# First column pair of the output projection as eight plain block products, and two norms turned with diagonal matrices

## The chip, the cores and the metric

The kernel runs on one core of one Trainium2 chip. The metric is the device time of one launch in microseconds; the median of three runs before the change is 2388.78 us (2388.70 to 2394.04).

The core's engines run their own queues in order and meet at semaphores: TensorE (PE, matrix products into PSUM), VectorE (DVE), ScalarE (ACT), GpSimd (POOL) and SyncE (SP, here only a queue of loads).

## The reference

One layer over 512 latent tokens of width 2048, with 256 context tokens that only feed the initial states of the scans. All arithmetic is float32.

```
mods      = silu(c) @ w_mod + b_mod                  # shift, scale, gate, twice
hx        = rmsnorm(x) * norm1_g * (1 + sc1) + sh1
q,k,v,g,… = hx @ w_in                                # heads of linear attention, and a short convolution
o         = bidirectional gated scan of q,k,v        # 4 heads, key 128, value 256, chunks of 64
mix[0:8]  = rmsnorm(o) * gla_norm_g * silu(g)        # norm over the 256 values of a head
mix[8:16] = B * conv3(C * x_in)
x1        = x + gt1 * (mix @ w_out)                  # the output projection, 2048 x 2048
h2        = rmsnorm(x1) * norm2_g * (1 + sc2) + sh2
out       = rmsnorm(x1 + gt2 * ((silu(h2 @ w_gate) * (h2 @ w_up)) @ w_down)) * final_g
```

## The kernel before

**Split products.** Every large float32 product is three products of two parts: `hi` is the value rounded to PE's faster float format (L102, a cast on ACT), `lo` is the rest (L103, a subtraction on DVE), and `mm3` adds lo·hi, hi·lo and hi·hi in PSUM. So each weight tile of 128 x 1024 (512 KB) costs one cast and one subtraction before PE may use it. The parts have three buffers each (`whi`, `wlo`); raw weights have four (`raw`, `load_raw`).

**First half: projections and scans.** `hx` is kept as 16 column tiles with their parts; the odd ones lie in the eight buffers tagged `ch`, the even ones in the 32 tagged `h`. `proj_units` multiplies one weight tile with eight of these, 24 matmuls, and yields. `do_q`, `do_g` and `do_conv` are built of such units. `do_gla(h)` is the scan of a head, cut by yields into steps. `weave` runs one step of the scan and one projection unit in turn until the scan is done, and then the rest of the units, so that PE always has a unit between two steps. After each unit `mod_some(MOD_STEP, 64)` adds 0.95 of a modulation row: a row is two loads of 512 KB through the `raw` buffers and two multiply-and-sum instructions on DVE (L373). The units of all `weave` calls are 74 steps. `mod_some(64, 64)` does what is left at the end, and `mod_finish` makes `modv`, from which the gates of the projections come (`cols_to_row`, two small turns on PE at L841).

At the end of a scan the norm of a head (L629 to L634) squares each 128 x 256 part of the output on ACT with a sum per row, makes the reciprocal root (`rsqrt_of_sum`, seven small instructions on DVE and ACT), and scales the parts with it on ACT. One yield later PE turns them in blocks of 128 x 128 (L639), tokens along the free axis, and DVE multiplies with `silu(g)` into `mix` (L641).

**Second half: products in seven.** The output projection and both FFN products multiply blocks by the Strassen-Winograd form: the left matrix is cut in four (`A11`, `A12`, `A21`, `A22`: token half and half of the inner dimension), the right one too, and seven products with sums of blocks take the place of eight. The left operands are `A11`, `A12`, `A22` and the sums `S1 = A21 + A22`, `S2 = S1 - A11`, `S3 = A11 - A21`, `S4 = A12 - S2`. `prep_a` makes and splits them, group after group. `seven` runs the products in steps named by block ("1", "5", "63", "7", "24"); `before` holds functions that are called ahead of a step. For each of four units of a product there are 12 matmuls of 128 x 512. `after` takes the finished sums. For the output projection `w_out` is two column pairs, `p = 0` and `p = 1`, and `prep_a` is called once, ahead of both; `take` multiplies by the gate row, adds `x`, squares for the second norm, and stores the sum to DRAM on POOL's queue. `load_x` loads the gate rows and `x` ahead of step "63".

The first half of the tokens is normalised before step "7" of the second pair (`half_a`), the second half after it: `norm2_scale` makes the root and scales eight tiles on ACT (L878), `norm2_back` turns them (L888, 32 turns of 128 x 128) and applies scale and shift on ACT (L893). The left operands of the FFN for the second half are made ahead of step "5" of the FFN's first block column, `j = 0` (`half_b`).

**Order and buffers.** The order on PE, DVE, ACT and POOL is set by a planner that takes instructions in the order of the text when its own costs say that their operands are ready; from the output projection on, SP's loads keep the order of the text. Tiles share buffers by tag: `t` (24 in `xpool`, where the 16 `mix` tiles lie too), `h` (32), `e` (17), `ch` (8); a tile waits for the last use of the one whose buffer it takes.

Of the kernel before, what the change touches and what calls it, by code (L numbers as in the profile page):

```python
# [7 lines left out]
F32 = mybir.dt.float32  # L8
# [5 lines left out]
P = 128  # L14
# [8 lines left out]
DV = 256  # L23
# [30 lines left out]
def tile_hybrid_block(  # L54
# [76 lines left out]
    def tok(t, tt):  # L131
        return t[:, tt * P : tt * P + P]
# [18 lines left out]
    def row_bcast(ps, pool, r):  # L151

        for tt in range(r.shape[-1]):
            dg = pool.tile([P, P], F32, tag="rb_d", name="rb_d", bufs=2)
            nc.vector.tensor_scalar(dg, ident, r[:, tt : tt + 1], None, op0=ALU.mult)
            mm(tok(ps, tt), ones, dg, tt == 0, True)


# [219 lines left out]

    MOD_STEP = 0.95

# [174 lines left out]
    def do_gla(h):  # L555
# [8 lines left out]
        for d in range(2):  # L564
# [64 lines left out]
        for tt in range(NX):  # L629
            nc.scalar.activation(on[:, tt, :], opart(tt), AF.Square, accum_out=ss[:, tt : tt + 1])  # L630
        r = rsqrt_of_sum(gp, ss, 1.0 / DV, NX)
        for tt in range(NX):
            nc.scalar.activation(on[:, tt, :], opart(tt), AF.Copy, scale=r[:, tt : tt + 1])
        yield  # L634

        for vh in range(2):
            pt = bank("pt")
            for tt in range(NX):
                nc.tensor.transpose(tok(pt, tt), on[:, tt, vh * P : vh * P + P], ident)  # L639
            m = mix[2 * h + vh]  # L640
            nc.vector.scalar_tensor_tensor(m, pt, col(C_GLA + vh), m, op0=ALU.mult, op1=ALU.mult)  # L641
# [48 lines left out]
    ctx.enter_context(tc.manual_schedule(engines={mybir.EngineType.SP}))  # L690
    A11, S1, S2, S4, S3, A12, A22 = range(7)

# [6 lines left out]
    def new_a(nk):  # L699

        return [[None] * (nk // 2) for _ in range(7)]

    def a_unit(A, i, u, spill=()):
        if A[i][u] is None:
            A[i][u] = tuple(fpool.tile([P, 2, HALF], F32R, tag="e", name=f"a{i}{p}", bufs=17) if (i, u) in spill else
                            xpool.tile([P, 2, HALF], F32R, tag="h" if i < 4 else "t", name=f"a{i}{p}",
                                       bufs=32 if i < 4 else 24) for p in "hl")
        return A[i][u]

    def prep_a(A, pieces, order, spill=()):  # L710


        tmp = {}
        tt = nc.vector.tensor_tensor

        def put(u, sel, i, src):
            hi, lo = a_unit(A, i, u, spill)
            split(hi[:, sel, :], lo[:, sel, :], src)

        def one(i, u, sel, a11, a12, a21, a22):  # L720
            if i == S1:
                if u not in tmp:
                    tmp[u] = row2k("s").rearrange("p (k t) -> p k t", k=2)
                tt(tmp[u][:, sel, :], a21(), a22(), op=ALU.add)
            elif i == S2:
                tt(tmp[u][:, sel, :], tmp[u][:, sel, :], a11(), op=ALU.subtract)
            elif i == S4:
                tt(tmp[u][:, sel, :], a12(), tmp[u][:, sel, :], op=ALU.subtract)
            if i == S3:
                t = row2k("s3").rearrange("p (k t) -> p k t", k=2)[:, sel, :]  # L730
                tt(t, a11(), a21(), op=ALU.subtract)
                put(u, sel, i, t)
            elif i in (S1, S2, S4):
                put(u, sel, i, tmp[u][:, sel, :])
            else:
                put(u, sel, i, {A11: a11, A12: a12, A22: a22}[i]())

        for group in order:
            for piece in pieces:
                for i in group if type(group) is tuple else (group,):  # L740
                    one(i, *piece)
            yield

    ALL_STEPS = ("1", "5", "63", "7", "24")

    def seven(A, wsrc, nk, after, steps=ALL_STEPS, before={}):
# [23 lines left out]
        for step in steps:  # L770
            if step in before:
                before[step]()
            for u in range(nu):
                end = u == nu - 1
                if step == "1":
# [36 lines left out]
    def sums(take, roomy=False):  # L812
# [18 lines left out]
        def direct(acc):  # L831
            for t in range(2):
# [23 lines left out]
    mx = lambda i, hf: (lambda: mix[i][:, hf * HALF : hf * HALF + HALF])  # L856
    for _ in prep_a(A, [(n // 2, n % 2, mx(k, 0), mx(l, 0), mx(k, 1), mx(l, 1)) for n, (k, l) in enumerate(zip(MIX1, MIX2))],
                    (A11, S1, S2, S4, S3, (A12, A22)), spill=((A22, 2), (A22, 3))):
        pass
    xn = [[None] * NBD for _ in range(NX)]  # L860
# [9 lines left out]

    raws, xs = {}, {}

    def norm2_scale(hf):
        r = row_scale(ssq, 2 * hf, 2)
        for d in range(NBD):
            for t in range(2):
                xs[2 * hf + t, d] = big() if hf else hbig()
                nc.scalar.activation(xs[2 * hf + t, d], xn[2 * hf + t][d], AF.Copy, scale=r[:, t : t + 1])  # L878
# [19 lines left out]
    rw = lambda hf, u: (lambda: raws[hf, u])  # L898
    gen = prep_a(A2, [(u, ALL, rw(0, u), rw(0, 4 + u), rw(1, u), rw(1, 4 + u)) for u in range(4)],
                 (A11, A12, S1, S2, S3, S4, A22))  # L900

    def half_a():
        norm2_scale(0)
        norm2_back(0)
        next(gen)
        next(gen)

    for p in range(NBD // 2):
# [19 lines left out]

        before = {"63": load_x}
        if p:  # L930
            before["7"] = half_a
        seven(A, lambda b, u: wo[p, b, u], 8, sums(take, True), ("1", "5", "63", "2", "7", "4") if p else ALL_STEPS, before)

# [5 lines left out]
    acts = {}  # L939

    def half_b():
        norm2_back(1)
        for _ in gen:
            pass

# [45 lines left out]
    for j in range(NPU):  # L991
# [15 lines left out]
        if j == 0:  # L1007
            steps, before = ("1", "2", "5", "63", "7", "4"), {"5": half_b}
        else:
# [199 lines left out]
```

## Time and profile before

| | |
|---|---|
| median of three runs | 2388.78 us (2388.70 to 2394.04) |
| profiled execution | 2393.07 us, its span 2391.3 us |
| mean granted clock of PE | 0.973 |
| busy in the span | PE 2252.2 us, DVE 1704.9, ACT 1030.8, POOL 136.3 |
| loads and stores | 431.42 MB, 180 GB/s on average |
| scans begin (first head's turn of k, L559) | 419.90 us |
| first matmul of the output projection | 849.45 us |
| first matmul of its second pair | 955.87 us |
| first matmul of the FFN, and of its second block column | 1053.46 and 1155.46 us |

Times within the profile count from the start of the span. A line of the waits says which engine's instruction stood idle for which, with the total, the number of times and the longest. A line of groups has the busy time, the mean length of one in ns, and the idle time in front. A line of the timeline has start and length; `x8` are eight instructions in a row, and brackets hold the idle time in front and what ended it. PE's rows overlap their neighbours, so the work of one is read from start to start. A product of two plain float32 operands leaves two rows.

### The profile page before, as it was taken

The numbers are of one execution on the slowest core, as the hardware profiler recorded it, in microseconds if no ns is written. First come the engines' busy times: TensorE is split into PE (matmuls) and PEld (weight loads), VectorE is DVE, ScalarE is ACT, GpSimd is POOL, SyncE is SP. The second block draws the span as 40 slices with busy tenths as digits, with TensorE's granted clock in tenths as the row PEclk, the third lists the DMA queues.
The fourth block names the chain that finished last, engine by engine and source line by source line (L and its number), as shares of the span: only waits on it lengthen the run. The fifth ranks groups of instructions, "written<-read, shape, count | busy, mean of one in ns | idle before, by whom it ended". The sixth has DMA issues, their size and how long they took to land.

```text
span 2391.3 us, 27558 instructions
## 1 busy us (share of the span) xinstructions
PE 2252.2 (94%) x10184; PEld 1793.0 (75%) x10184; DVE 1704.9 (71%) x2088; ACT 1030.8 (43%) x1391; POOL 136.3 (6%) x186
## 2 busy tenths in 40 slices
PE   8999999888979969987999999999999999999996
PEld 4765666777868747765888888888888878888875
DVE  3555165665665577768887888788877867787798
ACT  3422055322232344475445554555454544443343
POOL 2422000000000000000000000000000000000001
PEclk9999999999989989998999999999999999999998
DMA  9773466665766244541446434544354494855734
GB/s 326 229 253 111 150 228 194 199 213 187 231 192 217 90 150 128 178 157 52 145 150 203 143 128 145 193 150 142 139 176 159 165 362 151 289 185 178 255 130 141
DMA packets 161619, 431.42 MB, mean 180 GB/s; under 512 B 17867, under 2 KB 38635, under 8 KB 161356
## 3 DMA queue, kind: packets, MB, share of 16 engines
q1 hardware_dynamic: 141612, 380.87, 48.1%
q0 software_dynamic: 8720, 28.58, 3.2%
q10 hardware_dynamic: 11152, 20.21, 2.3%
q8 instruction: 80, 1.31, 0.2%
q14 instruction: 55, 0.45, 0.1%
HBM read 380.82 MB, written 48.78 MB: 180 GB/s over the span
## 4 chain that ended last, share of the span: by engine, by line
issue 57%; POOL 2%; PE 2%; DVE 0%; POOLq 0%; ACT 0%
PE acc L90 2%; POOL opd L971 2%; POOL out L1088 0%; POOL xnd L927 0%; ACT whi L102 0%; DVE xn L925 0%; POOLq L971 0%; DVE wlo L103 0%; DVE u L924 0%; DVE g L922 0%; DVE u L827 0%; POOLq L1205 0%; POOLq L1088 0%; POOLq L927 0%
## 5 line engine op out<-in xcount | busy, mean ns | idle before, releaser
L102 ACT CAST whi<-ch 128x1024 fp32r<-128x1024 f32 x370 | 390.2, 1056 | 461.5 <-PE acc L90 380.4
L103 DVE TENSOR_TENSOR wlo<-ch,whi 128x1024 fp32r<-128x1024 f32 x370 | 450.5, 1224 | 153.8 <-ACT whi L102 153.0
L102 ACT CAST whi<-raw 128x1024 fp32r<-128x1024 f32 x244 | 256.4, 1053 | 405.7 <-PE acc L90 284.9
L103 DVE TENSOR_TENSOR wlo<-raw,whi 128x1024 fp32r<-128x1024 f32 x244 | 302.5, 1240 | 158.8 <-ACT whi L102 158.1
L373 DVE CUSTOM_DVE_ANT_0 raw<-raw,cbc 128x1024 f32<-128x1024 f32 x128 | 156.3, 1224 | 159.6 <-DMA raw<-wm 157.2
L90 PE MATMUL acc<-hhl,whi 128*128 128x512 f32 x640 | 200.0, 393 | 0.0
L90 PE MATMUL acc<-hhi,wlo 128*128 128x512 f32 x320 | 133.4, 418 | 9.1 <-DVE wlo L103 8.3
L90 PEld LDWEIGHTS acc<-hhl,whi 128*128 128x128 f32 x640 | 121.1, 190 | 27.3 <-issue 2.5
L90 PE MATMUL acc<-wlo,a0h 128*128 128x512 f32 x296 | 117.5, 397 | 25.1 <-DVE wlo L103 25.1
L90 PE MATMUL acc<-hhl,wlo 128*128 128x512 f32 x320 | 127.5, 398 | 0.0
L90 PE MATMUL acc<-hlo,whi 128*128 128x512 f32 x320 | 127.2, 397 | 0.2 <-DVE hlo L108 0.2
L90 PE MATMUL acc<-hhi,whi 128*128 128x512 f32 x320 | 126.8, 396 | 0.0
L90 PE MATMUL acc<-whi,a1l 128*128 128x512 f32 x296 | 117.3, 398 | 9.6 <-DVE a1l L103 8.0
L90 PE MATMUL acc<-wlo,a1h 128*128 128x512 f32 x296 | 117.2, 396 | 9.5 <-DVE wlo L103 9.5
L90 PE MATMUL acc<-whi,a6l 128*128 128x512 f32 x296 | 116.4, 395 | 8.8 <-ACT whi L102 7.5
L90 PE MATMUL acc<-whi,a2l 128*128 128x512 f32 x296 | 116.1, 395 | 6.4 <-ACT whi L102 6.4
L90 PE MATMUL acc<-wlo,a2h 128*128 128x512 f32 x296 | 118.0, 399 | 0.9 <-DVE wlo L103 0.9
L90 PE MATMUL acc<-whi,a2h 128*128 128x512 f32 x296 | 117.8, 398 | 0.0
L90 PE MATMUL acc<-wlo,a6h 128*128 128x512 f32 x296 | 116.6, 394 | 0.9 <-DVE wlo L103 0.9
L90 PE MATMUL acc<-whi,a1h 128*128 128x512 f32 x296 | 116.9, 395 | 0.0
L90 PE MATMUL acc<-wlo,a3h 128*128 128x512 f32 x296 | 115.6, 391 | 1.1 <-DVE wlo L103 1.1
L90 PE MATMUL acc<-wlo,a4h 128*128 128x512 f32 x296 | 115.4, 390 | 1.2 <-DVE wlo L103 1.2
(310 smaller groups left out, 4802.8 us busy)
## 6 DMA issues: line engine op xcount, KB each, us to landing
raw<-wm SPq DMA_DIRECT2D x128, 512.0 KB, 4.7
raw<-wu SPq DMA_DIRECT2D x92, 512.0 KB, 4.5
ch<-wu SPq DMA_DIRECT2D x88, 512.0 KB, 3.8
raw<-wc SPq DMA_DIRECT2D x48, 512.0 KB, 3.7
raw<-wd SPq DMA_DIRECT2D x47, 512.0 KB, 6.4
ch<-wd SPq DMA_DIRECT2D x44, 512.0 KB, 6.0
opd<-oh ACTq DMA_DIRECT2D x77, 256.0 KB, 3.1
opd<-ol POOLq DMA_DIRECT2D x77, 256.0 KB, 3.3
```

Of the source, the lines that this page charges most:

```text
L90: nc.tensor.matmul(o, l, r, start=start, stop=stop, skip_group_check=True)
L102: nc.scalar.copy(hi, src)
L103: (eng or nc.vector).tensor_tensor(lo, src, hi, op=ALU.subtract)
L373: nc.vector.tensor_tensor_reduce(out=w, in0=w, in1=cbc[:, hf * 1024 : hf * 1024 + 1024], scale=1.0, scalar=0.0, op0=ALU.mult, op1=ALU.add, ...
L971: nc.gpsimd.dma_start(opd[j][i, 1].rearrange("p k t -> p (k t)"), lo.bitcast(F32))
```

## The change

- **Output projection, first pair.** `seven` with `p = 0` becomes `eight`: for each of the two columns, both halves of the inner dimension and four units, 24 matmuls into four banks. Its weights go through `raw`, where `seven` held the first two blocks in `ch`. The left blocks are made unit by unit (`hooks`): `A11` and `A21` ahead of the first half, `A12` and `A22` ahead of the second, and the sums for the second pair in the second column. `A21` and the raw sums lie in `ch`, `A12`, `A22` and `S2` in `h`, `S3`, `S4` and half of `S1` in `t`, the rest of `S1` in `e`.
- **Norm of a head.** The parts are copied to SBUF as they are and squared in place in PSUM. After a yield the root is made, and from it four diagonal matrices on DVE (`diagonals`); after two more yields PE multiplies the parts with them, which scales and turns at once.
- **Second norm.** The eight scaled copies of `norm2_scale` go; two diagonal matrices of a half take their place, and the turns of `norm2_back` become products with them. The second half's turns stand ahead of step "2" of `j = 0`, and its left operands are made unit by unit.
- `do_gla` yields once more before the scores (`psc`), and `MOD_STEP` is 0.85.

```diff
+    def diagonals(pool, r, bufs=4):
+        dgs = []
+        for tt in range(r.shape[-1]):
+            dg = pool.tile([P, P], F32, tag="dg", name="dg", bufs=bufs)
+            nc.vector.tensor_scalar(dg, ident, r[:, tt : tt + 1], None, op0=ALU.mult)
+            dgs.append(dg)
+        return dgs
...
-    MOD_STEP = 0.95
+    MOD_STEP = 0.85
...
             kes.append(ke)
             yield
+        yield
         for d in range(2):
             psc = bank("psc")
...
         for tt in range(NX):
-            nc.scalar.activation(on[:, tt, :], opart(tt), AF.Square, accum_out=ss[:, tt : tt + 1])
-        r = rsqrt_of_sum(gp, ss, 1.0 / DV, NX)
-        for tt in range(NX):
-            nc.scalar.activation(on[:, tt, :], opart(tt), AF.Copy, scale=r[:, tt : tt + 1])
+            nc.scalar.copy(on[:, tt, :], opart(tt))
+            nc.scalar.activation(opart(tt), opart(tt), AF.Square, accum_out=ss[:, tt : tt + 1])
+        yield
+        dgs = diagonals(gp, rsqrt_of_sum(gp, ss, 1.0 / DV, NX))
+        yield
         yield
...
-                nc.tensor.transpose(tok(pt, tt), on[:, tt, vh * P : vh * P + P], ident)
+                mm(tok(pt, tt), on[:, tt, vh * P : vh * P + P], dgs[tt], tt == 0, True)
...
+    def eight(A, wsrc, nk, take, before={}):
+        nu = nk // 2
+        for c in range(2):
+            acc = [[bank8("acc"), bank8("acc")] for _ in range(2)]
+            for kh in range(2):
+                for u in range(nu):
+                    if (c, kh, u) in before:
+                        before[c, kh, u]()
+                    hi = wpool.tile([P, 1024], F32R, tag="whi", name="whi", bufs=3)
+                    lo = wpool.tile([P, 1024], F32R, tag="wlo", name="wlo", bufs=3)
+                    split(hi, lo, load_raw(wsrc(2 * kh + c, u)))
+                    for hf in range(2):
+                        for t in range(2):
+                            for k in range(2):
+                                mm3(acc[hf][t], sl(A[((A11, A12), (A21, A22))[hf][kh]][u], ALL, k, slice(t * P, t * P + P)),
+                                    (hi[:, k * NB : k * NB + NB], lo[:, k * NB : k * NB + NB]),
+                                    kh == 0 and u == 0 and k == 0, kh == 1 and u == nu - 1 and k == 1)
+            for tt in range(NX):
+                take(tt, c, None, acc[tt // 2][tt % 2])
...
-    for _ in prep_a(A, [...], (A11, S1, S2, S4, S3, (A12, A22)), spill=((A22, 2), (A22, 3))):
-        pass
+    prep = preparer(A, pieces, lambda: wpool.tile([P, 2 * NB], F32, tag="ch", name="s", bufs=8)[:, :NB],
+                    lambda i, u: {A21: "ch", S1: "e" if u < 2 else "t", S3: "t", S4: "t"}.get(i, "h"))
...
     def norm2_scale(hf):
-        r = row_scale(ssq, 2 * hf, 2)
-        for d in range(NBD):
-            for t in range(2):
-                xs[2 * hf + t, d] = big() if hf else hbig()
-                nc.scalar.activation(xs[2 * hf + t, d], xn[2 * hf + t][d], AF.Copy, scale=r[:, t : t + 1])
+        dgs2[hf] = diagonals(fpool, row_scale(ssq, 2 * hf, 2), 3)
...
-            dst = row2k("h2") if hf else hbig()
+            dst = row2k("h2") if hf else big()
...
-                    nc.tensor.transpose(pt[:, (2 * kk + t) * P : (2 * kk + t) * P + P],
-                                        xs[2 * hf + t, k // 4][:, k % 4 * P : k % 4 * P + P], ident)
+                    mm(pt[:, (2 * kk + t) * P : (2 * kk + t) * P + P],
+                       xn[2 * hf + t][k // 4][:, k % 4 * P : k % 4 * P + P], dgs2[hf][t], kk == 0 and t == 0, True)
...
+        if p == 0:
+            before = hooks(prep, ((0, 0), (A11, A21)), ((0, 1), (A12, A22)), ((1, 0), (S1, S3)), ((1, 1), (S2, S4)))
+            first = before[0, 1, 0]
+            before[0, 1, 0] = lambda: (first(), load_x())
+            eight(A, w, 8, take, before)
+        else:
+            seven(A, w, 8, sums(take, True), ("1", "5", "63", "2", "7", "4"), {"63": load_x, "7": half_a})
...
         if j == 0:
-            steps, before = ("1", "2", "5", "63", "7", "4"), {"5": half_b}
+            steps = ("1", "2", "5", "63", "7", "4")
+            before = hooks(prep2, (("5",), (S1,)), (("63",), (S2, S4)), (("7",), (S3,)), (("4",), (A22,)))
+            before["2"] = lambda: norm2_back(1)
```

More of the change, by code (lines that the diff above doesn't have):

```diff
@@ L690, in tile_hybrid_block @@
     ctx.enter_context(tc.manual_schedule(engines={mybir.EngineType.SP}))
-    A11, S1, S2, S4, S3, A12, A22 = range(7)
+    A11, S1, S2, S4, S3, A12, A22, A21 = range(8)
     def bank8(name="bank8"):
@@ L699, in new_a, with a_unit @@
     def new_a(nk):
-        return [[None] * (nk // 2) for _ in range(7)]
-    def a_unit(A, i, u, spill=()):
+        return [[None] * (nk // 2) for _ in range(8)]
+    def a_unit(A, i, u, home=None):
         if A[i][u] is None:
-            A[i][u] = tuple(fpool.tile([P, 2, HALF], F32R, tag="e", name=f"a{i}{p}", bufs=17) if (i, u) in spill else
-                            xpool.tile([P, 2, HALF], F32R, tag="h" if i < 4 else "t", name=f"a{i}{p}",
-                                       bufs=32 if i < 4 else 24) for p in "hl")
+            home = home(i, u) if home else "h" if i < 4 else "t"
+            if home == "ch":
+                both = wpool.tile([P, 2, 2, HALF], F32R, tag="ch", name=f"a{i}", bufs=8)
+                A[i][u] = (both[:, 0], both[:, 1])
+            else:
+                pool, bufs = {"h": (xpool, 32), "t": (xpool, 24), "e": (fpool, 17)}[home]
+                A[i][u] = tuple(pool.tile([P, 2, HALF], F32R, tag=home, name=f"a{i}{p}", bufs=bufs) for p in "hl")
@@ L708, in a_unit, with preparer @@
         return A[i][u]
-    def prep_a(A, pieces, order, spill=()):
+    def preparer(A, pieces, sum_tile, home=None):
         tmp = {}
         tt = nc.vector.tensor_tensor
[L716 to L742, printed above, removed]
@@ new lines, in do @@
+        def do(u, *ops):
+            for i in ops:
+                hi, lo = a_unit(A, i, u, home)
+                if i == S1:
+                    tmp[u] = sum_tile().rearrange("p (k t) -> p k t", k=2)
+                t = row2k("s3").rearrange("p (k t) -> p k t", k=2) if i == S3 else tmp.get(u)
+                for sel, a11, a12, a21, a22 in pieces[u]:
+                    if i == S1:
+                        tt(t[:, sel, :], a21(), a22(), op=ALU.add)
+                    elif i == S2:
+                        tt(t[:, sel, :], t[:, sel, :], a11(), op=ALU.subtract)
+                    elif i == S4:
+                        tt(t[:, sel, :], a12(), t[:, sel, :], op=ALU.subtract)
+                    elif i == S3:
+                        tt(t[:, sel, :], a11(), a21(), op=ALU.subtract)
+                    else:
+                        split(hi[:, sel, :], lo[:, sel, :], {A11: a11, A12: a12, A21: a21, A22: a22}[i]())
+                if i in (S1, S2, S3, S4):
+                    split(hi, lo, t)
@@ L744, in tile_hybrid_block @@
+        return do
     ALL_STEPS = ("1", "5", "63", "7", "24")
@@ L773, in seven @@
             for u in range(nu):
+                if (step, u) in before:
+                    before[step, u]()
                 end = u == nu - 1
@@ L856, in tile_hybrid_block @@
     mx = lambda i, hf: (lambda: mix[i][:, hf * HALF : hf * HALF + HALF])
-    for _ in prep_a(A, [(n // 2, n % 2, mx(k, 0), mx(l, 0), mx(k, 1), mx(l, 1)) for n, (k, l) in enumerate(zip(MIX1, MIX2))],
-                    (A11, S1, S2, S4, S3, (A12, A22)), spill=((A22, 2), (A22, 3))):
-        pass
+    pieces = [[(n % 2, mx(MIX1[n], 0), mx(MIX2[n], 0), mx(MIX1[n], 1), mx(MIX2[n], 1)) for n in (2 * u, 2 * u + 1)]
+              for u in range(4)]
+    prep = preparer(A, pieces, lambda: wpool.tile([P, 2 * NB], F32, tag="ch", name="s", bufs=8)[:, :NB],
+                    lambda i, u: {A21: "ch", S1: "e" if u < 2 else "t", S3: "t", S4: "t"}.get(i, "h"))
     xn = [[None] * NBD for _ in range(NX)]
@@ L869, in row_scale @@
         return rsqrt_of_sum(fpool, s, 1.0 / D, n)
-    raws, xs = {}, {}
+    raws, dgs2 = {}, {}
     def norm2_scale(hf):
-        r = row_scale(ssq, 2 * hf, 2)
-        for d in range(NBD):
-            for t in range(2):
-                xs[2 * hf + t, d] = big() if hf else hbig()
-                nc.scalar.activation(xs[2 * hf + t, d], xn[2 * hf + t][d], AF.Copy, scale=r[:, t : t + 1])
+        dgs2[hf] = diagonals(fpool, row_scale(ssq, 2 * hf, 2), 3)
     def norm2_back(hf):
@@ L898, in tile_hybrid_block @@
     rw = lambda hf, u: (lambda: raws[hf, u])
-    gen = prep_a(A2, [(u, ALL, rw(0, u), rw(0, 4 + u), rw(1, u), rw(1, 4 + u)) for u in range(4)],
-                 (A11, A12, S1, S2, S3, S4, A22))
+    prep2 = preparer(A2, [[(ALL, rw(0, u), rw(0, 4 + u), rw(1, u), rw(1, 4 + u))] for u in range(4)], lambda: row2k("s"))
     def half_a():
@@ L904, in half_a, with hooks @@
         norm2_back(0)
-        next(gen)
-        next(gen)
+        for i in (A11, A12):
+            for u in range(4):
+                prep2(u, i)
+    def hooks(do, *at):
+        return {key + (u,): (lambda u=u, ops=ops: do(u, *ops)) for key, ops in at for u in range(4)}
     for p in range(NBD // 2):
@@ L927, in take @@
             nc.gpsimd.dma_start(xnd[tt, :, d * NB : d * NB + NB], xn[tt][d])
[L929 to L932, printed above, removed]
+        w = lambda b, u: wo[p, b, u]
+        if p == 0:
[3 more added lines that the diff above has]
+            eight(A, w, 8, take, before)
+        else:
+            seven(A, w, 8, sums(take, True), ("1", "5", "63", "2", "7", "4"), {"63": load_x, "7": half_a})
     norm2_scale(1)
@@ L939, in tile_hybrid_block @@
     acts = {}
[L941 to L944, printed above, removed]
     back_state = {}
```

## Prediction

> **What bounds the kernel now.** I read the page's first part, then who waited for whom on TensorE (PE) over the whole run: total, times, longest, in us.
>
> ```profile
> PE 2252.2 (94%) x10184; PEld 1793.0 (75%) x10184; DVE 1704.9 (71%) x2088; ACT 1030.8 (43%) x1391; POOL 136.3 (6%) x186
> PE acc L90 <- DVE wlo L103: 47.0, 16, 22.2
> PE pt L639 <- ACT on L633: 22.0, 3, 8.7
> PE acc L90 <- ACT whi L102: 15.9, 7, 7.5
> PE psc L90 <- DVE qe L578: 13.5, 4, 3.9
> PE psc L90 <- ACT a0h L102: 3.2, 1, 3.2
> ```
>
> PE is busy 94% of the span, so its own work is the bound, and only its idle time or fewer matmuls can pay. Next I cut the part that the diff touches at the first matmul of each stage (scans; first output pair; second; start of the FFN): window, length, then busy time (and count) of PE, PEld, DVE, ACT, POOL, then granted clock.
>
> ```profile
> 419.90:849.45 429.55, 390.36 (x1779) 325.06 (x1778) 252.65 (x424) 126.44 (x204) 0.00 (x0) 0.94 0.59 190
> 849.45:955.87 106.42, 80.80 (x339) 65.17 (x337) 88.23 (x142) 51.38 (x93) 2.32 (x4) 0.87 0.40 131
> 955.87:1053.46 97.59, 86.27 (x370) 68.62 (x368) 73.75 (x85) 54.98 (x87) 5.43 (x10) 0.93 0.55 181
> 1053.46:1131.00 77.54, 61.37 (x264) 49.99 (x263) 65.48 (x83) 50.49 (x77) 1.09 (x2) 0.87 0.19 61
> ```
>
> Idle PE is 39.2, 25.6, 11.3 and 16.2 us: 92 us, most of what the list above holds. The granted clock below 1.00 (third number from the end) says that PE also runs slowly after waits. The timeline of the first pair (start, length, engine, line, operation, out<-in, count, idle before) gives the unit of work and the long wait:
>
> ```profile
> 849.77 0.40 PE L90 MATMUL acc<-wlo,a0h 128*128 128x512 f32 x1
> 854.76 0.39 PE L90 MATMUL acc<-whi,a0h 128*128 128x512 f32 x1
> 880.07 0.80 PE L90 MATMUL acc<-wlo,a0h 128*128 128x512 f32 x1 [22.17 <-DVE wlo L103]
> ...
> 851.96 1.09 DVE L724 TENSOR_TENSOR s<-big 128x256 f32<-128x256 f32 x3
> 878.42 0.46 DVE L103 TENSOR_TENSOR a6l<-big,a6h 128x256 fp32r<-128x256 f32 x1
> 878.75 3.53 DVE L103 TENSOR_TENSOR wlo<-ch,whi 128x1024 fp32r<-128x1024 f32 x3
> ```
>
> 22 matmuls lie between the first two starts: 4.99 / 22 = 0.227 us each. The wait of 22.17 us is VectorE (DVE) making six of the seven sets of left operands, 851.96 to 878.75, ahead of the weight splits.
>
> The scans wait otherwise. Rows of the third head (DVE, then PE), with the fourth head's turn at 821 that waited for nothing, and L373's windows:
>
> ```profile
> 703.02 0.16 DVE L142 TENSOR_SCALAR rs_m<-ss 128x4 f32<-128x4 f32 x1
> 708.76 1.23 DVE L373 CUSTOM_DVE_ANT_0 raw<-raw,cbc 128x1024 f32<-128x1024 f32 x1 [5.58 <-DMA raw<-wm]
> 711.50 2.43 PE L639 MATMUL pt<-cidt,on 128*128 128x128 f32 x8 [8.74 <-ACT on L633]
> 821.20 1.03 PE L639 MATMUL pt<-cidt,on 128*128 128x128 f32 x8
> 659.62 2.05 PE L90 MATMUL psc<-qe,ke 128*128 128x128 f32 x8 [3.47 <-DVE qe L578]
> 664.74 2.05 PE L90 MATMUL psc<-qe,ke 128*128 128x128 f32 x8 [3.08 <-DVE qe L578]
> 641.00:764.00 123.00, 39.41 (x64) 0.92 0.64 203
> 800.00:850.00 50.00, 0.00 (x0) 1.00 0.24 78
> ```
>
> The norm's short chain sits on DVE between modulation multiplies (L373), and one of those waited 5.58 us for its own load. So PE waits for a DMA that it does not need. The last two rows count L373's records (two per multiply): 32 multiplies in the third head's 123 us, none after 800, where the turn waited for nothing.
>
> **The change, part by part.**
>
> **Scans (419.90 to 849.45).** One more empty step before the scores, and two more between norm and turn. Each puts one projection unit in front of the waiting PE instruction: 24 matmuls x 0.227 = 5.4 us of cover. The scores were late by at most 3.9 us each, about 7 us for a head's pair (13.5 in two heads); the turn was late by up to 8.74 with one unit of cover and now gets three, so 10.9 more, against which the diagonals add DVE work. That work is unseen; it lies between a 128x4 and a 128x512 tensor_scalar:
>
> ```profile
> L147 DVE TENSOR_SCALAR rs_t<-rs_t 128x4 f32<-128x4 f32 x3 | 0.5, 170 | 0.1
> L653 DVE TENSOR_SCALAR big<-big,colt 128x512 f32<-128x512 f32 x6 | 2.9, 485 | 0.1
> L633 ACT ACTIVATE on<-po,rs_r 128x256 f32<-128x256 f32 x12 | 4.7, 475 | 13.7 <-DVE rs_r L148 13.7
> 519.19 0.60 PE L559 MATMUL pk<-cidt,big 128*128 128x128 f32 x4
> 519.63 1.06 PE L90 MATMUL pcm<-cstt,hbig 128*128 128x128 f32 x8
> 520.52 1.06 PE L90 MATMUL psf<-hbig,cstt 128*128 128x128 f32 x8
> ```
>
> Four diagonals cost 0.7 to 1.9 us; nearer the small one, 1.0. On ScalarE (ACT) four scaled copies of 0.48 become plain ones and the squares remain: nothing, and the copies now end before the reciprocal root instead of behind it. The turn as fp32 matmul: four transposes take 519.63 - 519.19 = 0.44, four fp32 products (two records each) 0.89, so +0.11 each; 32 here make +3.5. The pacing of 0.85 thins the loads by a tenth: a head's step has 2.7 loads of 512 KB instead of 2.9, which shortens the DVE's waits for them.
> Removable: 39.2 idle, and the slow tail. Eight transposes took 2.43 instead of 1.03, and the scores' tails are alike; about 2 to 2.5 us for each of six late places, 15. I let a quarter of 54 stay (head three's second score started 664.74 - 656.15 = 8.6 us after the first could have, and the cover is 5.4): -40.5 + 3.5 = **-37**. Ends: +3.5 (no wait goes) and -51.
>
> **First pair (849.45 to 955.87).** 7 products x 4 units x 12 = 336 matmuls become 384: 384 x 0.227 = 87.1 us, against 106.4 now. DVE must keep up: the old block was 26.8 us, another set (A21) is 8 x 0.36 (1.09 for three), sixteen splits at 1.14 (3.53 for three, overlapped ends) are 18.2, and two sets of takes about 10: 58 of 87 us, made unit by unit in front of the split that needs them. It fits. The start is worse: 74 steps x 0.85 finish 62 of 64 modulation rows, where 0.95 finished all at the 68th. Two rows, four loads, now stand on SP's queue ahead of the first output weight, which has moved to the four raw buffers. Head three loaded 32 halves of rows and 16 weights in 123 us, one in 2.6 us, so 10 us, and splits run about two units (10.9) ahead: 0 to 5 late, I take 3. The two small turns of the gate rows wait for the same last row, and load_x's ten loads stand ahead of the ninth block's weight with four units (21.8 us) of cover: nothing. The second pair's held weights wait on SP for the buffers of A21 and of the sums, given back unit by unit in the second column block, 43.6 us ahead: nothing. The takes of the first block lie beside the second block's matmuls, and POOL's stores follow them as before. 87.1 + 3 - 106.4 = **-16**. Ends: -19 (no delay) and +6 (the 22.2 us wait comes back with its 3 us tail).
>
> **Second pair (955.87 to 1053.46).** The first half's norm loses eight scales on ACT:
>
> ```profile
> 1026.30 2.56 ACT L878 ACTIVATE hbig<-xn,rs_r 128x512 f32<-128x512 f32 x4
> 1031.22 7.37 ACT L893 ACTIVATE hbig<-pt,modv,gsc 128x256 f32<-128x256 f32 x16
> 1044.94 1.22 PE L90 MATMUL acc<-whi,a6l 128*128 128x512 f32 x2 [7.51 <-ACT whi L102]
> 1064.09 0.15 DVE L148 TENSOR_TENSOR rs_r<-rs_r,rs_t 128x2 f32<-128x2 f32 x1
> 1087.43 0.80 PE L90 MATMUL acc<-whi,a1l 128*128 128x512 f32 x1 [8.03 <-DVE a1l L103]
> 1106.86 0.80 PE L90 MATMUL acc<-wlo,a1h 128*128 128x512 f32 x1 [8.07 <-DVE wlo L103]
> 1155.46 0.39 PE L90 MATMUL acc<-whi,a0l 128*128 128x512 f32 x1
> ```
>
> ACT is the chain here: scales from 1026.30, the shift-and-scale from 1031.22. The 4.9 us between go, and 32 turns x 0.22 = 7.0 us of PE work fill the wait of 7.51. The stage's PE work is 336 x 0.227 + 7.0 = 83.3; I leave 7 us of its small waits: 90.3 - 97.6 = **-7**. Ends: +3.5 and -14.
>
> **Start of the FFN (1053.46 to 1155.46, 102 us).** The turn of the second half moves from before the third product to before the second, and its scales go; the root is ready at 1064.09, the second product starts 10.9 us after 1053.46. So the shift-and-scale ends some 9 us earlier, and the sums are made per unit. Two waits of 8 stand there, and DVE remains full behind them, so I leave 6 us: 83.3 + 6 - 102 = **-13**. Ends: +3.5 and -19.
>
> Sum: -37 - 16 - 7 - 13 = -73. The profiled execution took 2393.07 (span 2391.3 and 1.8 around it), 4.3 over the median of 2388.78. 2393.1 - 73 = **2320**. Extremes: 2290 and 2410.
>
> One rule against it: the Trainium skill, "TensorE: Matmul & The Clock Gate", section "Terms", says that the transpose mode is four times faster for fp32. By that each of the 96 turns would cost 0.33 more instead of 0.11, and the sum would be 21 us worse; the rows here show a factor of two for 128x128.
>
> **Rivals.**
> *The scans keep their waits* (2360). The load stream, not the order, would pace them: 203 GB/s in head three. For: one multiply waited 5.58 us. Against: from 800 on, no multiplies and no wait. Then +3.5 instead of -37: 2320 + 40.
> *The left sums still run as a block ahead of the weight splits* (2342), since the planner orders DVE and ACT by its own costs: the change does not do what it says. Then the first pair gives +6 instead of -16.
> *A diagonal product costs four transposes, 0.44, not two* (2341): PE passes then weigh more in 96 turns, 96 x 0.22. Against: the pcm and psf rows. The Trainium skill's page named above would have it so.
> *Slower: the 24 "t" slots.* Sixteen mixed tiles hold 16 of 24 until the sums are made; sums S1, S3, S4 want 20 in the second column block. The queue has waited for such a slot already:
>
> ```profile
> SPq L849 <- DVE a6l L103: 28.3, 1, 28.3
> ```
>
> If ACT's cast waits for a slot in front of the weight casts, PE waits too. One such wait of 28.3 still gives 2348; it decides from the third (68.8 / 28.3 = 2.4): 2320 + 85 = 2405. Against: a slot pair comes free with each unit's own subtraction, and S1 is needed only 10.9 us into the next pair.
>
> **How the numbers follow.** Forecast 0.68, waits in scans 0.13, block of sums 0.12, costly turns 0.03, slots 0.04. The time is the forecast's. The range leaves out the scans' rival and the slower one and part of the lower end: 2298 (two thirds of the way to all ends) to 2354. A change under 0.3% (7 us; the three runs lie 5.3 apart) can't be told from none. Faster 0.93, the same 0.03, slower 0.04.
>
> **What would show it.** Right: no wait for psc or the turn over 3 us; 384 matmuls in about 90 us without a 22 us gap; the first output weight's wait under 5 us; no wait over 3 us before the A22 product; j = 0 in about 90 us. Wrong: waits of DVE for modulation loads as long as now with PE behind them, a new gap in the second column block, or a long one where the scans end and the last modulation rows land.

## The result, and the profile after

The changed kernel takes 2353.98 us (median of four runs, 2347.83 to 2357.13) where the kernel before takes 2391.41 beside it: ratio 0.9843, 95% interval 0.9828 to 0.9858, faster by 37 us. The prediction said 2320 with a range of 2298 to 2354. The sign was right, the gain a little more than half of the one forecast, and the time lies 0.02 us inside the upper end of the range. For 2354 the prediction gives no sum, so that it still covers the result is luck. The profiled execution after has a span of 2353.8 us, 37.5 less than before, and a mean granted clock of 0.986.

First part of the page after, and PE's waits over the whole run (what it waited for; total, times, longest, in us):

```profile
PE 2270.1 (96%) x10328; PEld 1807.0 (77%) x10328; DVE 1671.7 (71%) x2066; ACT 1002.5 (43%) x1349; POOL 136.1 (6%) x186
PE acc L90 <- DVE wlo L103: 24.3, 20, 3.3
PE pd L90 <- DVE hbig L606: 9.0, 4, 4.1
PE po L90 <- ACT sm L620: 5.8, 9, 1.5
PE acc L90 <- ACT whi L102: 5.0, 3, 3.1
PE psc L90 <- DVE ke L589: 4.2, 1, 4.2
PE acc L90 <- DVE big L838: 2.6, 1, 2.6
PE acc L90 <- DVE big L671: 2.5, 1, 2.5
```

PE has 144 matmul records more and is busy for 18 us more, and still the span is shorter: the wait of 22 us and the two of 8 are gone, of the one of 7.5 2.6 are left, and the wait of the heads' turns (22.0 before) is gone too. New is a wait of `pd`, a product within the scan, for DVE's masked copy (L606 after): it was not on the list before.

The same stages as before, cut at the first matmul of each (scans; first pair; second pair; first block column of the FFN); below them the last one of the kernel before, cut anew because the prediction's window stopped at 1131:

```profile
422.13:846.39 424.26, 395.46 (x1812) 324.66 (x1810) 263.00 (x463) 131.00 (x226) 0.00 (x0) 0.97 0.62 196
846.39:937.98 91.59, 89.06 (x387) 73.25 (x385) 53.42 (x91) 30.33 (x47) 3.08 (x6) 0.98 0.48 158
937.98:1031.27 93.29, 87.71 (x402) 71.94 (x400) 70.33 (x84) 49.62 (x77) 4.63 (x9) 0.96 0.57 189
1031.27:1116.89 85.62, 84.53 (x401) 69.79 (x400) 80.92 (x102) 54.99 (x79) 1.09 (x2) 1.00 0.36 113
```

```profile
1053.46:1155.46 102.00, 85.46 (x370) 69.62 (x368) 81.45 (x100) 60.59 (x87) 1.09 (x2) 0.90 0.31 99
```

| stage | before | after | difference | predicted |
|---|---|---|---|---|
| until the scans begin | 419.90 | 422.13 | +2.2 | 0 |
| scans | 429.55 | 424.26 | -5.3 | -37 |
| first pair | 106.42 | 91.59 | -14.8 | -16 |
| second pair | 97.59 | 93.29 | -4.3 | -7 |
| FFN, j = 0 | 102.00 | 85.62 | -16.4 | -13 |
| the rest | 1235.84 | 1236.91 | +1.1 | 0 |
| sum | 2391.3 | 2353.8 | -37.5 | -73 |

The three stages behind the scans gave 35.5 of the 36 us forecast for them, in part because the second pair's shortfall of 2.7 us and the 3.4 us that `j = 0` gave beyond its forecast cancel. Of the 35.5 us that are missing in the sum, 31.7 lie in the scans, where the idle time of PE fell from 39.2 us only to 28.8. Waits inside the scans, of DVE for the rows of the modulation weight and of SP for a buffer to load into, first before, then after:

```profile
DVE raw L373 <- DMA raw<-wm: 126.9, 67, 5.6
SPq L118 <- DVE modacc L373: 212.8, 86, 5.4
```

```profile
DVE raw L382 <- DMA raw<-wm: 157.5, 74, 5.7
SPq L118 <- DVE modacc L382: 232.8, 82, 6.5
```

Both grew. Four rows of the timeline after show what became of them in the fourth head (start, length, engine, operation, and in brackets the idle time before):

```profile
786.80 1.23 DVE L382 CUSTOM_DVE_ANT_0 raw<-raw,cbc 128x1024 f32<-128x1024 f32 x1 [1.44 <-DMA raw<-wm]
789.57 1.23 DVE L382 CUSTOM_DVE_ANT_0 raw<-raw,cbc 128x1024 f32<-128x1024 f32 x1 [0.87 <-DMA raw<-wm]
790.72 1.33 DVE L606 COPY_PREDICATED hbig<-maskt,psc 128x512 f32<-128x512 uint8 x2
791.50 2.07 PE L90 MATMUL pd<-vx,kk 128*128 128x256 f32 x4 [4.12 <-DVE hbig L606]
```

DVE waits for a load, multiplies, waits for the next load, multiplies, and only then makes the copy that PE has stood 4.12 us for. It is the picture that the prediction drew for the turn, at another place.

### The profile page after: what moved, and what is told of

It is laid out like the page before. It is cut to its first block, busy times and chain, and to the rows that moved or that the text cites. A ratio compares the mean times of both kernels' runs of the same rounds, so it can differ in the third digit from the quotient of the medians.

```text
span 2353.8 us, 27801 instructions
## 1 busy us (share of the span) xinstructions
PE 2270.1 (96%) x10328; PEld 1807.0 (77%) x10328; DVE 1671.7 (71%) x2066; ACT 1002.5 (43%) x1349; POOL 136.1 (6%) x186
## 4 chain that ended last, share of the span: by engine, by line
PE 50%; DVE 5%; DMA 2%; issue 1%; ACT 1%; SPq 0%; POOL 0%; DVEq 0%; POOLq 0%; ACTq 0%
PE acc L90 49%; DVE wlo L103 2%; DMA raw<-wd 1%; PE pt L990 1%; DMA raw<-wu 1%; PE pt L90 1%; DVE y L1102 0%; DVE y L1122 0%; ACT whi L102 0%; DVE ch L818 0%; DVE y L1114 0%; DMA ch<-wd 0%; DVE y L1113 0%; DVE ch L799 0%; DVE hbig L959 0%
## 5 line engine op out<-in xcount | busy, mean ns | idle before, releaser
L102 ACT CAST whi<-ch 128x1024 fp32r<-128x1024 f32 x350 | 368.7, 1054 | 433.4 <-PE acc L90 361.2
L103 DVE TENSOR_TENSOR wlo<-ch,whi 128x1024 fp32r<-128x1024 f32 x350 | 425.9, 1221 | 139.2 <-ACT whi L102 138.1
L102 ACT CAST whi<-raw 128x1024 fp32r<-128x1024 f32 x252 | 264.4, 1051 | 438.8 <-PE acc L90 250.5
L103 DVE TENSOR_TENSOR wlo<-raw,whi 128x1024 fp32r<-128x1024 f32 x252 | 312.0, 1239 | 168.4 <-ACT whi L102 167.8
L90 PE MATMUL acc<-hhi,wlo 128*128 128x512 f32 x320 | 135.5, 425 | 17.8 <-DVE wlo L103 17.1
L90 PE MATMUL acc<-whi,a6h 128*128 128x512 f32 x312 | 122.6, 393 | 0.0
L90 PE MATMUL acc<-wlo,a5h 128*128 128x512 f32 x312 | 121.7, 390 | 0.9 <-DVE wlo L103 0.9
L90 PE MATMUL acc<-whi,a0h 128*128 128x512 f32 x312 | 122.3, 392 | 0.0
L90 PE MATMUL acc<-whi,a0l 128*128 128x512 f32 x312 | 121.8, 391 | 0.0
L90 PE MATMUL acc<-whi,a5l 128*128 128x512 f32 x312 | 121.5, 389 | 0.0
L90 PE MATMUL acc<-whi,a5h 128*128 128x512 f32 x312 | 121.5, 389 | 0.0
```

The costliest lines, as they stand in the source:

```text
L90: nc.tensor.matmul(o, l, r, start=start, stop=stop, skip_group_check=True)
L102: nc.scalar.copy(hi, src)
L103: (eng or nc.vector).tensor_tensor(lo, src, hi, op=ALU.subtract)
```

## The experiments

Theory after the result: *the loads of the modulation rows, not the order of the steps, hold up the scans*, and a wait removed at one place comes back at another. Rivals: DVE is short of time for the multiplies; only the head of DVE's queue does the harm; the cover was simply not long enough.

**No rows, multiplies alone, loads alone.** Three kernels that take the stream apart in `mod_some`.

```diff
 x_nomod:    -  both loads and both multiplies of a row
 x_noload:   -  w = load_raw(wm2[j][:, ...])
             +  w = wpool.tile([P, 1024], F32, tag="raw", bufs=4)   # multiply cbc by cbc into it
 x_loadonly: -  nc.vector.tensor_tensor_reduce(out=w, ...)
             +  nc.gpsimd.tensor_copy(modacc[:, j, hf : hf + 1], w[:, 0:1])
```

> The changed kernel without the modulation rows: neither their 128 loads nor their 128 multiplies are issued, and the sums are set to zero. Stage of the scans (first head's turn of k to the first output matmul) is 424.3 us in the changed kernel, with 28.8 us of idle PE and about 24 us of slow matmuls. Theory A (the scans are paced by the modulation stream: four raw buffers shared with the weights, loads in one queue, multiplies that wait for their loads at the head of VectorE's queue): the new waits for pd, po and wlo go, the stage falls to 375-390 us. Rival B (the new waits are of the change's own making: the longer cut of the scan, PSUM banks held longer, costlier turns): the stage stays at 412 us or more.

> The changed kernel with all 128 modulation multiplies but without their loads: each multiplies one resident half of the row of c with the other, and still takes a raw buffer for its result. If VectorE's own time for the multiplies is the price, the stage of the scans stays near 424 us; if the waits for the loads are (theory A), it falls to 375-395 us; rival B again 412 us or more.

> The changed kernel with all 128 modulation loads through the raw buffers, but without the multiplies: GpSimd reads one column of each instead. VectorE waits for no load any more. If the harm is done at the head of VectorE's queue, the stage of the scans falls to 380-395 us and the waits of PE for pd, po and the second psc go; if the harm is done on the load queue (weights late behind rows that wait for a buffer, or bandwidth), waits for wlo stay and the stage stays above 405 us.

Measured, one run each: 2296.6, 2294.8 and 2354.9 us. The windows of the scans, in this order (here and below they end at the small turn of the gate rows, up to 0.14 us ahead of the first matmul of the output projection):

```profile
415.68:793.32 377.64, 377.64 (x1809) 318.73 (x1808) 151.11 (x266) 132.68 (x226) 0.00 (x0) 1.00 0.25 78
414.47:792.12 377.65, 377.65 (x1810) 318.97 (x1808) 263.91 (x458) 132.56 (x226) 0.00 (x0) 1.00 0.25 79
418.35:853.74 435.39, 392.69 (x1809) 325.22 (x1808) 151.22 (x270) 132.41 (x226) 33.12 (x97) 0.95 0.57 187
```

Without loads PE does not wait once in the scans (its busy time fills the window, clock 1.00), and it makes no difference whether DVE multiplies (263.9 us busy) or not (151.1). With the loads and without a multiply on DVE the scans are 11 us longer than with it. So 46.6 us of the 424.26 hang on the loads alone; DVE's time is not the price, nor, alone, the multiply that waits at the head of its queue. With the loads alone the queue of loads itself shows it, and PE's waits change their place again:

```profile
SPq L118 <- DMA raw<-wm: 320.9, 97, 6.1
PE acc L90 <- DVE wlo L103: 26.9, 7, 18.5
ACT whi L102 <- DMA raw<-wc: 180.5, 34, 9.1
DVE modv L389 <- POOL modacc L382: 20.5, 1, 20.5
```

The weight that PE needs next stands on SP's queue behind loads that wait for a buffer: ACT's casts wait 180.5 us for weights of the convolution, where they wait 37.1 in the changed kernel. The single wait of 18.5 us, at the end of the scans, is something else. There DVE stood for 20.5 us at the sum of the rows in `mod_finish` until the last rows had landed, and the split that PE needed stood behind it. Taken off, it leaves some 417 of the 435.39 us, still 39 more than without loads.

**Two more buffers.** The rows get two buffers of their own beside the four of the weights; to make room only one column of `c` is kept, and all columns are multiplied by it.

```diff
-                w = load_raw(wm2[j][:, hf * 1024 : hf * 1024 + 1024])
+                w = epool.tile([P, 1024], F32, tag="rawm", name="rawm", bufs=2)
+                nc.sync.dma_start(w, wm2[j][:, hf * 1024 : hf * 1024 + 1024])
```

> The changed kernel with two buffers of their own for the modulation rows beside the four raw ones of the weights (room is made by keeping one column of the row of c, broadcast in the multiply, so the modulation values are others; loads, multiplies and their lengths stay). If too few buffers pace the stream, the stage of the scans falls to 385-410 us and the stretch moves more GB/s; if the 196 GB/s of the scans are all that the loads can get, it stays at 420-428 us.

Measured, one run: 2335.2 us; the scans begin 6.8 us later, at 428.92, and take 404.63. Three stretches of 50 us (the first begins 9 us ahead of the scans):

```profile
420.00:470.00 50.00, 45.80 (x220) 37.83 (x219) 36.47 (x63) 15.07 (x21) 0.00 (x0) 0.97 0.73 240
570.00:620.00 50.00, 47.39 (x209) 38.82 (x208) 32.87 (x56) 14.37 (x26) 0.00 (x0) 0.97 0.72 235
670.00:720.00 50.00, 50.00 (x241) 42.29 (x239) 18.34 (x32) 16.42 (x30) 0.00 (x0) 1.00 0.26 82
```

The last column is GB/s: 232 to 240 while there are rows, where four buffers moved 181 to 203 in every such stretch. So the four buffers, not the memory, held the stream at about 196. And as soon as the rows are through, PE is busy for 50.00 of 50.00 us. While they last it still waits.

One thing must be kept apart here. The rows begin with the first `weave`, ahead of the scans' window, so not all of them fall into it. The records of their multiplies, four to a row, count those that do; in the changed kernel (window, length, DVE's busy time with these multiplies and their records, clock, DMA share, GB/s):

```profile
422.13:846.39 424.26, 121.98 (x198) 0.97 0.62 196
```

That is 49.5 rows, with 14.5 ahead of the window. With six buffers 31 of the 64 rows are multiplied ahead of it and 33 inside, so a part of what the window gains is that fewer rows are left in it. The total, 19 us below the changed kernel's, holds without that reading.

**The order alone.** One kernel takes back the three new yields, one the pacing.

```diff
 x_yields:  -        yield          # ahead of the scores, and the two around the diagonals
 x_step95:  -    MOD_STEP = 0.85
            +    MOD_STEP = 0.95
```

> The changed kernel without the extra yields: none ahead of the scores, one instead of three between the norm and the turn. The prediction's step (each yield is 5.4 us of cover for a wait that then does not come back elsewhere) gives about 25 us more, 2380, and the waits for psc and the turn return. The theory that the modulation loads pace the scans, found by leaving them out (the stage fell from 424 to 378 us), says that it hardly matters where PE waits: the stage stays within 8 us of 424.

> The changed kernel with MOD_STEP back at 0.95. The prediction's step (fewer loads per unit shorten VectorE's waits) gives 5 to 10 us more. The theory that each modulation load inside the scans costs about 0.4 us of PE time (46.5 us for about 112 loads) whatever their spacing, gives the same number of loads and so 424 plus or minus 4 us for the stage, with a calm end after the last row.

Measured: 2359.93 us, ratio 0.9873 (0.9854 to 0.9892), scans 434.90; and 2358.35 us, ratio 0.9866 (0.9850 to 0.9883), scans 432.10. Waits in the scans of the first:

```profile
PE pt L90 <- DVE dg L163: 18.6, 4, 7.5
PE psc L90 <- DVE qe L587: 10.8, 5, 4.8
PE psc L90 <- DVE ke L589: 6.4, 1, 6.4
PE acc L90 <- DVE wlo L103: 2.3, 1, 2.3
```

Without the yields the waits of the turn and of the scores are back, 38 us with one more of 2.1, while `wlo` has 2.3 left and `pd` is not on the list. With the yields 5.3 of the 38 stay, and `pd`, `wlo` and `po` have 23.4 (9.0, 8.6 and 5.8 within the scans): most of the waits moved rather than went. Taken back alone, the yields cost the scans 10.6 us and the pacing 7.8; the two do not add up, since the whole change gave 5.3. Neither theory fits. The prediction's step wanted 25 us more for the yields and 5 to 10 for the pacing, and 6 and 4 were measured; the theory of the loads wanted the scans within 8 and within 4 us of 424. So beside the loads the order of the steps is worth something, but less than the prediction thought. These differences of 6 and 4 us lie at the edge of what the intervals tell from the changed kernel's 0.9828 to 0.9858.

**The first pair undone.** `seven` with its block of sums ahead, the rest as changed.

```diff
-            eight(A, w, 8, take, before)
+            seven(A, w, 8, sums(take, True), ALL_STEPS, {"63": load_x})
```

> The changed kernel with the first column pair undone: seven products, all left sums made and split ahead in the old order, load_x at step 63. All else stays changed. The prediction's step (the first pair is worth 16 us; the traces show 91.6 against 106.4 us for the stage) gives about 2354 + 15 = 2369 us and a wait of about 22 us of PE for wlo ahead of the second left unit. Rival: other stages take up the difference, the whole stays within 5 us of the changed kernel.

Measured: 2367.48 us, ratio 0.9900 (0.9879 to 0.9920), 13.5 us above the changed kernel. The pair takes 105.15 us instead of 91.59, with the old wait:

```profile
PE acc L90 <- DVE wlo L103: 20.2, 1, 20.2
```

**The second norm, in two parts.** One kernel scales the first half on ACT and turns it by transposes again; one puts the second half's turn back in front of step "5".

```diff
 x_scales:  -        dgs2[hf] = diagonals(fpool, row_scale(ssq, 2 * hf, 2), 3)
            +        if hf: dgs2[hf] = ...                       # as changed
            +        else:  xs[t, d] = hbig(); ACT Copy with scale, then transposes
 x_back5:   -            before["2"] = lambda: norm2_back(1)
            +            before["5"] = lambda: norm2_back(1)
```

> The changed kernel with one part undone: the first half of the second norm is scaled by eight copies on ACT and turned by transposes, as before; the second half keeps its diagonals. Theory (ACT's chain ends the stage): the 4.9 us of scales come back ahead of the turn, PE has 32 x 0.1 = 3.3 us less to do, the wait at the last left operand grows from 2.6 to 7 or more; second pair 93.3 + 1 to + 5 = 94 to 98 us, total within 0.2% of the changed kernel (2354 to 2359). Rival (PE's own work sets the stage, the scales are hidden): the second pair gets shorter by about 3 us, 90, total 2351.

> The changed kernel with one part undone: in the FFN's first block column the turn of the second half stands ahead of the third product again instead of the second; the sums stay unit by unit and the diagonals stay. Theory (the earlier place of the turn took away the waits): one product is 10.9 us, so waits of 6 to 11 us come back ahead of the products that need the second half, FFN j = 0 85.6 + 6 to 11 = 92 to 97 us, total 2360 to 2365. Rival (the unit-by-unit sums did it, the place costs nothing): j = 0 within 88 us, total 2354 to 2356.

Measured: 2358.86 us, ratio 0.9862 (0.9834 to 0.9889), which can't be told from the changed kernel's; and 2361.43, ratio 0.9878 (0.9858 to 0.9897). By stages: with the scales back the second pair takes 94.93 us instead of 93.29; with the later turn `j = 0` takes 91.62 instead of 85.62. Their rows, one of each:

```profile
1027.64 1.22 PE L90 MATMUL acc<-whi,a6l 128*128 128x512 f32 x2 [7.51 <-ACT whi L102]
```

```profile
1063.15 0.76 PE L90 MATMUL acc<-whi,a1l 128*128 128x512 f32 x1 [4.16 <-DVE a1l L103]
```

The wait of 7.51 us is that of the kernel before, to the hundredth: ACT's scales cause it, and they are worth 1.6 us here, since PE has 3.3 less to turn. The place of the turn is worth 6.0 of the 16.4 us of `j = 0`, at the lower end of the 6 to 11 expected; the other 10.4 are left for the sums made unit by unit and the scales of the second half, which were not tried apart.

**Rows moved ahead of the scans.** If the number of rows in the scans is the price, the value projections, before the scans, can take some: 16 (6 in the first, 10 in the second), or 24 (10 and 14), and with 16 ahead the 16 rows of the second gate can go into the FFN, whose loads have room. For this the row of `c` is loaded ahead of the value projections, and in the last kernel the second gate's row is made behind the block columns.

```diff
 x_early:    +        if i >= 10: mod_some(1, 64)     # first value projection
             +        if i < 10:  mod_some(1, 64)     # second one
             -    MOD_STEP = 0.85
             +    MOD_STEP = 0.65
 x_early24:  as x_early with i >= 6, i < 14 and MOD_STEP = 0.54
 x_late:     as x_early with MOD_STEP = 0.43, mod_some(MOD_STEP, 48), and in j = 1 to 8
             +  before["1", 0], before["7", 0]: two loads of 512 KB of the last 16 rows
             +  before["1", 3], before["7", 3]: their multiplies
```

> The changed kernel with 16 of the 64 modulation rows taken out of the scans: six are worked off in the last units of the first value projection and ten in the second one, where the loads move 22 to 200 GB/s and VectorE is busy for 3 to 17 us of 25; the pace of the rest is 0.65 rows a step. If a load inside the scans costs about 0.4 us and there is room for it ahead, 32 loads fewer give 13 us less: 2341 us, the stage of the scans 405 to 412. Rival: the value projections become as late as the scans become early, the whole stays within 4 us of the changed kernel.

> As x_early, but 24 rows ahead of the scans instead of 16 (10 in the first, 14 in the second value projection), MOD_STEP 0.54, 40 rows in the scans. Theory of the number of loads: scans 377.6 + 40 x 0.56 = 400 us, 4.4 less than x_early, and the scans' start stays at 421.8 if the value projections still have room: 2326. Rival (the value projections are full: they moved 240 to 263 GB/s in x_early): the scans' start slips by more than 4 us, to 426 or later, and the total is 2330 or above.

> As x_early (16 modulation rows loaded and multiplied inside the value projections), and the 16 rows of the second gate moved out of the scans too, into block columns 1 to 8 of the FFN as quarters of 512 columns; MOD_STEP 0.43, so 32 rows are left in the scans. Theory (what a scan pays is for the number of 512 KB loads that share its four buffers): 62 rows took 424.1 us, 48 took 404.4, none took 377.6, so 32 rows take 377.6 + 32 x (404.4 - 377.6) / 48 = 395.5 us, 9 us less than x_early, and the FFN, which has idle load time, hides the rest: 2330 - 9 = about 2321. Rival (the loads cost the same wherever they stand, since the FFN's weights go through the same buffers): the scans give 9 us and the FFN takes 9 or more back in waits of PE for wlo: 2330 or above. Rival two (the remaining price is one of single places, not of the number): scans above 402.

Measured, the windows of the scans with 48, 40 and 32 rows left to the `weave` calls, and the multiplies of rows within the window of the second:

```profile
421.78:826.20 404.42, 386.83 (x1810) 319.58 (x1809) 231.81 (x414) 131.77 (x226) 0.00 (x0) 0.99 0.53 169
438.33:818.70 380.37, 378.75 (x1810) 318.37 (x1808) 221.46 (x393) 132.65 (x226) 0.00 (x0) 1.00 0.52 165
423.55:801.20 377.65, 377.65 (x1809) 318.73 (x1808) 206.25 (x366) 132.91 (x226) 0.00 (x0) 1.00 0.47 148
```

```profile
438.33:818.70 380.37, 75.22 (x122) 1.00 0.52 165
```

| kernel | us | ratio, interval | rows in the `weave` calls | of these in the window | scans |
|---|---|---|---|---|---|
| changed | 2353.98 | 0.9843 (0.9828 to 0.9858) | 62, and 2 behind them | 49.5 | 424.26 |
| x_early | 2330.2 | 0.9748 (0.9733 to 0.9763) | 48 | 36 | 404.42 |
| x_early24 | 2320.97 | 0.9708 (0.9688 to 0.9729) | 40 | 30.5 | 380.37 |
| x_late | 2337.31 | 0.9777 (0.9756 to 0.9797) | 32 | 24 | 377.65 |

The expectations count the rows of the `weave` calls as rows in the scans; the window holds fewer, as the table says. The theory's sign holds and its straight line does not: 36 rows in the window cost 26.8 us over the scans without loads, 30.5 cost 2.7, 24 nothing. x_early came out better than its 2341 and 405 to 412 us: 27 loads fewer in the window gave 19.8 us, 0.73 each and not 0.4, and the first pair gave 4.5 more. With 30.5 rows DVE still waits for them, 58 times, and PE no longer does (four waits, 1.6 us in all):

```profile
DVE raw L353 <- DMA raw<-wm: 137.3, 58, 5.6
PE po L90 <- ACT sm L624: 1.6, 4, 0.9
```

So the waits of DVE are no measure of the loss; whether they reach PE is. Both numbers that I expected of x_early24 failed: the scans' start did slip, by 16.2 us, as the rival had it, but the scans gave 43.9 and the total fell below x_early's. x_late missed its total of 2321: the scans were better than expected, and the FFN took back more than they gave, as the first rival had it. From the scans' end to the end of the span x_early needs 1500.7 us and x_late 1537.0. In x_late, from 1067 to 1720, DVE waits for the moved rows and PE for its splits and casts:

```profile
DVE raw L1047 <- DMA raw<-wm: 36.9, 24, 3.6
PE acc L90 <- DVE wlo L103: 11.6, 12, 2.1
PE acc L90 <- ACT whi L102: 8.6, 4, 2.1
```

In x_early PE's waits in the same stretch come to 0.9 us. So a load that PE does not need costs also there. Whether by DVE's wait for it ahead of a split that PE does need, or by the shared buffers, was not tried apart for the FFN. Open stays as well why 36 rows in the window, at 169 GB/s, make PE wait and 30.5, at 165, hardly do. x_early24 beats both kernels, 33 us below the changed one.

## Why the prediction was right and wrong

**Scans: -37 predicted, -5.3 measured. This step failed.** The forecast of 2320 failed here and nearly nowhere else. It took the idle time as so many late instructions, each of which a unit of 5.4 us in front would cover, and let a quarter stay. The cover worked where it was put: the turn's 22.0 us are gone and the scores' 16.7 fell to 5.3. But the waits came back at `pd` (9.0), at `wlo` and at `po` (5.8), since the scans move their loads at 190 GB/s before and 196 after, as fast as four buffers let them. What is removable was sized well: my lower end of -51 is what leaving out the loads gives, 377.64 - 429.55 = -51.9. What it took was fewer rows in the stage, and only in part another order (10.6 and 7.8 us, when the yields or the pacing are taken back). The sentence that the pacing "shortens the DVE's waits" for loads was wrong: 126.9 us became 157.5, and with the pacing alone taken back they are 144.3. With PE behind them, that is the first sign of being wrong that the prediction itself named; and a wait for the scores of 4.2 us (`ke`) stands where it allowed 3. The rival that named the load stream had the mechanism, and its 2360 is 6 us from the 2353.98 measured, where the forecast is 34 away; its argument against, that from 800 on nothing waited, was in truth one for it, since there were no rows left by then. It got 0.13 where the rows of 203 GB/s and 5.58 us deserved more, and its +3.5 was off too, as pacing and yields did give some. (A slip of arithmetic beside it: two thirds of the way from 2320 to 2290 is 2300, not 2298.)

**First pair: -16, measured -14.8.** 87.1 us of matmuls plus 3 for a late start; 91.59 was measured. The late start is there, as a wait of 2.53 us, but not by the first weight:

```profile
849.82 1.42 DVE L739 TENSOR_TENSOR s<-big 128x256 f32<-128x256 f32 x4
851.16 0.68 DVE L671 TENSOR_TENSOR big<-big,acc 128x512 f32<-128x512 f32 x1
851.90 0.50 PE L90 MATMUL acc<-whi,a 128*128 128x512 f32 x1 [2.53 <-DVE big L671]
```

L671 is the last product of a convolution. Its operand from PE was there by 846.5, but on DVE splits of left blocks and, of the sums for the second pair, four stood ahead of it. So the planner did put some of the left sums early, as the rival of the block of sums feared; PE waits 2.5 us there, and not 22. In x_early and x_early24 the pair takes 87.14 and 87.13: the first term was exact. The wait for slots did not come: in the two pairs no wait of PE is over 2.6 us.

**Second pair: -7, measured -4.3.** The wait of 7.51 became 2.59 as said; 7 us of small waits were allowed for; all waits, the 2.59 among them, came to 5.6 us and the slow matmuls after them to 4.4.

**Start of the FFN: -13, measured -16.4.** The rows behind the turn after:

```profile
1020.29 0.80 PE L90 MATMUL acc<-whi,a6l 128*128 128x512 f32 x1 [2.59 <-DVE big L838]
1042.53 3.81 PE L90 MATMUL pt<-dg,xn 128*128 128x128 f32 x32 [0.22 <-DVE dg L163]
```

Both waits of 8 us are gone, and of the 6 us that I left for them 2.3 were needed: 85.62 against 83.3 of work. DVE, 80.92 us busy in 85.62, kept up.

**Price of a turn: right.** Eight fp32 products of a head, two records each, took 1.95 us where eight transposes took 1.03:

```profile
496.98 1.95 PE L90 MATMUL pt<-dg,on 128*128 128x128 f32 x16
```

That is 0.12 more for each, 0.11 predicted. The rule of the Trainium skill that the prediction weighed against it, a transpose mode four times faster for fp32 ("TensorE: Matmul & The Clock Gate", "Terms"), would make it 0.33, an estimate from the 0.11 us of one transpose. These rows show a factor of two, and none names the mode.

## What to carry to other kernels

When several waits of one stage all end on the same stream of loads, size the stage by that stream and not by the waits: cover put in front of one place moves the wait to the next. Take the stream away in a trial first; what remains is the true floor, and the number of loads that still fits under it is found by moving some out, here 40 of 64 rows, of which 30.5 fall into the stage. A block of work ahead of a stage that PE waits for as a whole is different: making it in pieces next to its use gave what was worked out, within 2 us.

## What the runs showed of the hardware

A wait costs more than its length. The scans have the same matmuls with and without loads, and PE's busy time for them was 395.46 us with 28.8 us of waits and 377.64 with none: 17.8 us, 0.6 for each us of waiting, are slower matmuls. With the loads alone, where the waits were fewer and longer (42.7 us, one of them of 18.5), it was 15.1 us or 0.35. The timeline after shows one such place:

```profile
616.23 0.50 PE L90 MATMUL acc<-hhi,wlo 128*128 128x512 f32 x1 [2.46 <-DVE wlo L103]
...
618.41 0.63 PE L90 MATMUL acc<-hhi,wlo 128*128 128x512 f32 x1
618.84 0.63 PE L90 MATMUL acc<-hlo,whi 128*128 128x512 f32 x1
...
620.90 0.39 PE L90 MATMUL acc<-hlo,whi 128*128 128x512 f32 x1
621.13 0.39 PE L90 MATMUL acc<-hhi,whi 128*128 128x512 f32 x1
```

After a wait of 2.46 us the first matmuls start 0.23 to 0.34 us apart, from 617.13 on 0.43 for some 3 us (granted clock 0.52 up to 620.40), and 0.23 apart again from 620.67 on. The Trainium skill, "TensorE: Matmul & The Clock Gate", section "What's actually happening", puts the half clock behind an idle window of about 3.4 us; here a shorter wait was enough.

And a shared ring of buffers bounds a stream well below what the memory gives: four buffers of 512 KB, each load landing 4.7 us (median) after its issue, moved 181 to 203 GB/s in the scans, six moved 232 to 240.
